# The opening of a decoder layer on one core: partial sums copied back into PSUM, every pair of tiles turned by transfers, conditioning one group earlier, x loaded by features, rows on GpSimd's queue

## The chip, the cores and the metric

The kernel runs on one core of one Trainium2 chip. The metric is the device time of one execution in microseconds. Engines are named as in the profile: PE is TensorE (matmuls and transposes), PEld its weight loads, DVE is VectorE, ACT is ScalarE, POOL is GpSimd and SP is SyncE, which issues most of the transfers. L12 is line 12 of the kernel.

## The reference

One layer: an adaLN-conditioned SwiGLU, token mixing (retention and sliding-window attention side by side), a second SwiGLU and a last norm, for 256 tokens of 2048 features, all in float32. The change touches the conditioning and the first SwiGLU:

```python
c_act = jax.nn.silu(c)
mod = (c_act @ w_ada[l] + b_ada[l]).reshape(b, N_MOD, D_MODEL)       # nine vectors of 2048
h = modulate(rms_norm(x, norm_ffn1[l]), mod[:, 0], mod[:, 1])         # h * (1 + scale) + shift
gate, up = jnp.split(h @ w_gu, 2, axis=-1)                            # w_gu: 2048 x 11264
x = x + 0.5 * mod[:, 2][:, None, :] * ((jax.nn.silu(gate) * up) @ w_down)
```

## The kernel before, in words

**Products.** A float32 product is made of three products of a shorter float type: the high part of the weights times the high part of the activations, high times low, and low times high (`products`, L349 to L363). ACT casts a weight tile to its high part (`wh`, L369), DVE subtracts that from the tile to get the low part (`wl`, L371). Both come two blocks at a time, 128x1024 numbers, into pools of three buffers each. The tiles themselves (`raw`, four buffers) are loaded by SP. Activations `h` are kept as `hh` (cast by ACT, L630) and `hl` (DVE, L631).

**The opening.** The first SwiGLU needs `h`, and `h` needs the conditioning vectors 0 and 1, which are products of silu(c) with 1 MB rows of `w_ada` (a row is a pair of vector number m and feature block k). The features are 16 blocks of 128. Rather than wait for all rows, the kernel begins with 16 chunks of 512 columns (eight pairs of a gate chunk and an up chunk) and goes over them in four groups of feature blocks: blocks 0 to 1, 2 to 5, 6 to 11 and 12 to 15 (L1114). Within a group every chunk is visited once (`visit`), which takes 12 matmuls for each two blocks. The order of the chunks is turned around in each group, and the last two chunks of a group keep their PSUM banks into the next. All others move their sums out: `to_parts` writes them to `part_of(n)` in SBUF, at the first time with an ACT copy (L1158), later with a DVE addition (L1155). In the last group `swiglu_up` adds the kept sums to the bank (L699, L700) and makes silu(gate) x up. The result is turned, for even pairs by PE transposes (L512) and an ACT copy (L513), for odd ones by two `flat` copies (L529), a transposing transfer (L534) and two copies back (L545). There are three `flat` buffers.

**What runs beside.** While the visits of one group run, the generator `group` prepares the blocks of the next: it loads rows (`place`, two row buffers in `ring` after the first rows), multiplies and sums them on DVE (`ada_pass`, L219: 128x2048 at once in the first group, two halves of 128x1024 later), ends the sums (`ada_end`, L237 to L244), scales x (`turned_x`, ACT, L1022), turns it by four PE transposes for each pair of blocks (L1026), modulates it (ACT, L622) and splits it into `hh` and `hl`. In the last group the rows of vectors 2, 4 and 3 begin (`set_pace`, 32 of their 192 quarter-row passes, 128x512 each); the rest follow in `ffn_up`.

**What sets the order.** Every engine takes its instructions in order. Which order that is follows from the program and from a scheduler, which places an instruction when it expects its inputs; `tc.issue_after` ties a copy to the newest cast. An instruction that waits holds up all behind it on its engine, and SP and POOL hold up the transfers behind a waiting one in the same way.

The pools that decide when buffers come free are these:

```python
raws = ctx.enter_context(tc.tile_pool(name="raws", bufs=RAWS))
wsp = ctx.enter_context(tc.tile_pool(name="wsp", bufs=3))
flat = ctx.enter_context(tc.tile_pool(name="flat", bufs=3))
psa = ctx.enter_context(tc.tile_pool(name="psa", bufs=4, space=PSUM))
psm = ctx.enter_context(tc.tile_pool(name="psm", bufs=2, space=PSUM))
psd = ctx.enter_context(tc.tile_pool(name="psd", bufs=2, space=PSUM))
```

A visit takes two banks of `psa`, so two chunks are in PSUM at a time.

## Time and profile before

| | |
|---|---|
| median of three runs | 2361.56 us (2360.13 to 2361.72) |
| the profiled execution | 2360.87 us, its span 2359.1 us |
| granted clock in the span | 0.999 |
| ACT, busy in the span | 1314.8 us |
| rows of `w_ada` loaded into `slot` buffers by SP | 83 of 1024 KB, median 7.0 us to landing |
| weight tiles of the SwiGLUs, by SP | 160 of 1024 KB, median 5.1 us to landing |

The opening is the first 450 us or so. A line of the windows view gives, for one stretch, the busy time of each engine with its count of instructions, then the granted clock of PE, the busy share of the DMA engines and what they moved. A line of the waits view gives the waiting instruction, who released it, and the total, the count and the longest of such waits. A line of the timeline gives start and duration, and in brackets the idle time before it with its releaser. In the chain, a line is a piece of the path that ended last.

### The profile page before, as it was taken

What the parts mean: (1) busy time and instruction counts of PE and PEld (TensorE: products, weight loads), DVE (VectorE), ACT (ScalarE), POOL (GpSimd) and SP (SyncE); (2) the same over time, 40 slices, a digit from 0 to 9 for tenths busy, and PEclk for the clock granted to TensorE, in tenths of its full rate; (3) what the DMA queues carried; (4) which work ended last, traced back from release to release, by engine and by line L of the source; (5) the groups of instructions that cost most, each with busy time, mean ns of one, the idle gap of its engine ahead of it and who ended that gap; (6) DMA issues with size and microseconds to landing.
All of it is one profiled execution on the core that took longest, in us unless ns stands there. A gap on an engine that the chain in (4) does not pass through costs nothing.

```text
span 2359.1 us, 28364 instructions
## 1 busy us (share of the span) xinstructions
PE 2338.8 (99%) x10479; PEld 1921.2 (81%) x10479; DVE 1697.5 (72%) x2628; ACT 1314.8 (56%) x1779; POOL 9.2 (0%) x21
## 2 busy tenths in 40 slices
PE   8999999999999999999999999999999999999998
PEld 5888888888888888778888888888888888888887
DVE  7987799779977768976777776676555555555656
ACT  6544466455556568774556564465455455455544
POOL 0000000000000000000000000000000000000000
PEclk9999999999999999999999999999999999999999
DMA  9987789999776889967678787754777777676553
GB/s 386 365 295 267 267 288 366 368 315 357 304 257 229 284 274 247 260 216 250 265 283 301 284 300 289 279 205 179 255 234 256 244 241 254 235 230 203 193 196 125
DMA packets 186316, 627.87 MB, mean 266 GB/s; under 512 B 108801, under 2 KB 109185, under 8 KB 115649
## 3 DMA queue, kind: packets, MB, share of 16 engines
q1 hardware_dynamic: 183682, 615.05, 74.9%
q0 software_dynamic: 1600, 9.83, 1.2%
q8 instruction: 82, 1.34, 0.2%
q10 hardware_dynamic: 896, 1.19, 0.1%
q14 instruction: 56, 0.46, 0.1%
HBM read 597.16 MB, written 4.22 MB: 255 GB/s over the span
## 4 chain that ended last, share of the span: by engine, by line
PE 97%; DMA 1%; DVE 1%; ACT 0%; issue 0%; SPq 0%; DVEq 0%; ACTq 0%
PE pa L355 95%; PE ps L1372 0%; DMA slot<-in_w_ada_dram 0%; DMA rows_x<-in_w_ada_dram 0%; PE pd L1288 0%; DVE slot L219 0%; DMA x_sb<-in_x_dram 0%; PE ps L355 0%; PE ps L888 0%; DVE wl L371 0%; PE ps L512 0%; ACT wh L369 0%; DVE rows_x L219 0%; PE ps L1288 0%; PE pd L1470 0%
## 5 line engine op out<-in xcount | busy, mean ns | idle before, releaser
L369 ACT CAST wh<-raw 128x1024 fp32r<-128x1024 f32 x792 | 831.1, 1054 | 883.3 <-PE pa L355 836.7
L371 DVE TENSOR_TENSOR wl<-raw,wh 128x1024 fp32r<-128x1024 f32 x792 | 960.8, 1222 | 478.0 <-ACT wh L369 416.6
L355 PE MATMUL pa<-wh,hh 128*128 128x512 f32 x2184 | 595.5, 392 | 2.2 <-ACT wh L369 1.6
L355 PE MATMUL pa<-wh,hl 128*128 128x512 f32 x2184 | 589.7, 389 | 0.0
L355 PE MATMUL pa<-wl,hh 128*128 128x512 f32 x2184 | 585.2, 390 | 0.4 <-DVE wl L371 0.3
L355 PEld LDWEIGHTS pa<-wh,hh 128*128 128x128 f32 x2184 | 407.3, 188 | 90.2 <-ACT wh L369 4.2
L355 PEld LDWEIGHTS pa<-wh,hl 128*128 128x128 f32 x2184 | 409.9, 188 | 86.3 <-issue 0.4
L355 PEld LDWEIGHTS pa<-wl,hh 128*128 128x128 f32 x2184 | 409.1, 188 | 87.0 <-DVE wl L371 1.3
L355 PE MATMUL pa<-wh,a 128*128 128x512 f32 x1824 | 452.4, 389 | 0.0
L355 PEld LDWEIGHTS pa<-wh,a 128*128 128x128 f32 x1824 | 341.6, 188 | 71.0 <-DVE a L405 0.4
L355 PE MATMUL pa<-wl,a 128*128 128x512 f32 x912 | 245.2, 389 | 0.0
L219 DVE CUSTOM_DVE_ANT_0 slot<-slot,cact 128x512 f32<-128x512 f32 (+2 forms) x272 | 209.5, 820 | 11.0 <-DMA slot<-in_w_ada_dram 10.8
L355 PEld LDWEIGHTS pa<-wl,a 128*128 128x128 f32 x912 | 171.1, 188 | 35.4
L219 DVE CUSTOM_DVE_ANT_0 rows_x<-rows_x,cact 128x512 f32<-128x512 f32 x124 | 78.8, 688 | 24.9 <-DMA rows_x<-in_w_ada_dram 24.9
L545 ACT COPY slot<-back 128x512 uint16<-128x512 uint16 x140 | 93.4, 767 | 0.0
L404 ACT CAST a<-slot 128x512 fp32r<-128x512 f32 x114 | 70.5, 620 | 28.3 <-PE pa L355 28.2
L219 DVE CUSTOM_DVE_ANT_0 raw<-raw,cact 128x512 f32<-128x512 f32 (+1 forms) x108 | 70.8, 708 | 20.3 <-DMA raw<-in_w_ada_dram 20.3
L405 DVE TENSOR_TENSOR a<-slot,a 128x512 fp32r<-128x512 f32 x114 | 78.0, 685 | 0.1
L529 ACT COPY flat<-t 128x512 uint16<-128x512 uint16 x128 | 72.1, 617 | 7.5 <-DVE t L1445 5.5
L1155 DVE TENSOR_TENSOR slot<-slot,pa 128x512 f32<-128x512 f32 x48 | 31.0, 683 | 16.7 <-PE pa L355 16.7
L219 DVE DVE_READ_ACCUMULATOR2_ANT sums<- 128x1 f32 x504 | 41.7, 83 | 0.0
L355 PE MATMUL pa<-wh,home 128*128 128x512 f32 x160 | 39.5, 389 | 0.0
(223 smaller groups left out, 1068.9 us busy)
## 6 DMA issues: line engine op xcount, KB each, us to landing
raw<-in_w_ffn_gu_dram SPq DMA_DIRECT2D x160, 1024.0 KB, 5.1
raw<-in_w_in_dram SPq DMA_DIRECT2D x104, 1024.0 KB, 6.4
raw<-in_w_ffn_down_dram SPq DMA_DIRECT2D x88, 1024.0 KB, 4.9
slot<-in_w_ada_dram SPq DMA_DIRECT2D x83, 1024.0 KB, 7.0
rows_x<-in_w_ada_dram SPq DMA_DIRECT2D x31, 1024.0 KB, 7.2
raw<-in_w_ada_dram SPq DMA_DIRECT2D x26, 1024.0 KB, 6.5
raw<-in_w_swa_branch_dram SPq DMA_DIRECT2D x16, 1024.0 KB, 6.1
raw<-in_w_ret_branch_dram SPq DMA_DIRECT2D x16, 1024.0 KB, 6.2
```

What stands on the lines that cost most here:

```text
L219: nc.vector.tensor_tensor_reduce(out=w[:, at], in0=w[:, at], in1=cact[:, at], scale=1.0, scalar=0.0, op0=ALU.mult, op1=ALU.add, accum_out= ...
L355: product = nc.tensor.matmul(banks[t], act[:, j, t * P : (t + 1) * P], weights[:, j, :], start=starts and i == 0 and j == 0, stop=ends and ...
L369: cast.append(nc.scalar.copy(hi, src).ins)
L371: low.append(nc.vector.tensor_sub(lo, src, hi.bitcast(F32)).ins)
L404: nc.scalar.copy(hi, v)
L405: nc.vector.tensor_sub(lo, v, hi.bitcast(F32))
L529: nc.scalar.copy(planes[:, i, :], words(src)[:, :, i])
L545: nc.scalar.copy(into[:, :, :, i], held["turned"][:, i])
L1155: nc.vector.tensor_add(p, p, b)
```

## The change

Five parts. (1) *Copied sums.* A chunk whose sums lie in SBUF has its two banks filled by ACT copies before its visit (seeds, L1172), the matmuls accumulate onto them, and `to_parts` always writes out with ACT copies; the additions of L1155 are gone. Chunks that are left to the last group are still added in `swiglu_up`. (2) All eight pairs are turned by transfers. (3) The 32 passes of vectors 2, 4 and 3 stand in the third group, with one row buffer for them, and the rows of the group itself then have one buffer too. (4) From block 6 on, x comes from a second copy of the input, laid out by features on the host (`x_t`); DVE multiplies it by the row of inverse norms (L1060), which one small matmul spreads over the partitions (L1053). (5) Rows of block 2 and up, and those of part 3, are loaded from GpSimd's queue.

```diff
@@ -207,11 +208,11 @@
 
     AQ = 4
 
-    def ada_load(m, k, w, loads=1):
+    def ada_load(m, k, w, loads=1, queue=nc.sync):
         src = w_ada[(m * KD + k) * P : (m * KD + k + 1) * P, :]
         for i in range(loads):
             at = slice(i * D // loads, (i + 1) * D // loads)
-            nc.sync.dma_start(w[:, at], src[:, at])
+            queue.dma_start(w[:, at], src[:, at])
 
     def ada_pass(k, w, sums, q, passes=AQ):
 
@@ -258,6 +259,10 @@
 
         return place
 
+    own_sums = [
+        small_c[:, C_COS : C_COS + KD * AQ].rearrange("p (k q) -> p k q", q=AQ)
+    ]
+
     def conditioning(outputs, place, behind):
 
 
@@ -265,13 +270,13 @@
         held = {}
         step = 0
         for m, gain, row in outputs:
-            sums = ada_sums()
+            sums = own_sums.pop() if own_sums else ada_sums()
             for k in range(KD):
                 for q in range(AQ):
                     for i in range(step // AQ, min((step + pace["ahead"]) // AQ + 1, len(tiles))):
                         if i not in held:
                             held[i] = place()
-                            ada_load(*tiles[i], held[i])
+                            ada_load(*tiles[i], held[i], 1, pace["queue"])
                     if behind is not None and step < 2 * AQ:
                         with tc.issue_after(behind.ins):
                             ada_pass(k, held[step // AQ], sums, q)
@@ -301,7 +306,7 @@
         return nc.gpsimd.dma_start(row, gate_d[m // 3][None, :].broadcast_to([P, D]))
 
 
-    pace = {"steps": iter(()), "rate": 0.0, "due": 0.0, "behind": None}
+    pace = {"steps": iter(()), "rate": 0.0, "due": 0.0, "behind": None, "queue": nc.gpsimd}
 
     def set_pace(outputs, halves, place, ahead):
         assert next(pace["steps"], None) is None
@@ -346,7 +351,7 @@
         nc.sync.dma_start(raw, w[c0 // CH, :, kb * KB : (kb + 1) * KB, :])
         return raw
 
-    def products(banks, ah, al, wh, wl, starts, ends, halves=range(NT)):
+    def products(banks, ah, al, wh, wl, starts, ends, halves=range(NT), seeded=False):
         n = ah.shape[1]
         parts = ((ah, wh), (al, wh), (ah, wl))
         for i, (act, weights) in enumerate(parts):
@@ -358,6 +363,7 @@
                         weights[:, j, :],
                         start=starts and i == 0 and j == 0,
                         stop=ends and i == 2 and j == n - 1,
+                        skip_group_check=seeded,
                     )
         newest.append(product.ins)
         del newest[:-1]
@@ -969,15 +975,19 @@
         return [part[(n - 2) // 4][:, at + t * CH : at + (t + 1) * CH] for t in range(NT)]
 
     early = [ada_sums() for _ in range(2)]
-    rows_of = {}
+    rows_of, alone = {}, [False]
 
     def place(m, k):
         if k < 1:
             rows_of[m, k] = raw_row()
         else:
-            ring.append(ring.pop(0))
-            rows_of[m, k] = ring[-1]
-        ada_load(m, k, rows_of[m, k], 2 if k < 2 else 1)
+            if not alone[0]:
+                ring.reverse()
+            rows_of[m, k] = ring[0]
+        if k < 2:
+            ada_load(m, k, rows_of[m, k], 2)
+        else:
+            ada_load(m, k, rows_of[m, k], 1, nc.gpsimd)
 
     firsts = (2 * EARLY - 1, 2 * EARLY - 2)
 
@@ -1028,9 +1038,34 @@
                 )
         return turned
 
+    TURNED = 6
+    root_rows = []
+
+    def roots_in_rows():
+
+        diag = t512()
+        for t in range(NT):
+            nc.scalar.mul(diag[:, t * P : (t + 1) * P], ident, r[:, t : t + 1])
+        full = flat_tile()[:, :P]
+        nc.gpsimd.memset(full, 1.0)
+        root_rows.append(side_bank()[:, :S])
+        with tc.issue_after(newest[-1]):
+            nc.tensor.matmul(root_rows[0], full, diag[:, :S], start=True, stop=True)
+
+    def normed_columns(k0):
+
+        xt = t512()
+        both = xt.rearrange("p (k s) -> p k s", s=S)
+        nc.sync.dma_start(both, x_t[k0 : k0 + 2].rearrange("k p s -> p k s"))
+        nc.vector.tensor_mul(
+            both, both, root_rows[0][:, None, :].broadcast_to([P, 2, S])
+        )
+        return [xt[:, i * S : (i + 1) * S] for i in range(2)]
+
     def group(ks, passes=2):
 
         for k0 in ks[::2]:
+            srcs = normed_columns(k0) if k0 >= TURNED else None
             for k in (k0, k0 + 1):
                 for m in (1, 0):
                     if (m, k) not in rows_of:
@@ -1041,11 +1076,11 @@
             for m in (1, 0):
                 ada_end(m, slice(k0, k0 + 2), early[m], 0 if m else None, passes)
             h = t512()
-            for i, src in enumerate(turned_x(k0)):
+            for i, src in enumerate(srcs or turned_x(k0)):
                 modulated(h[:, i * S : (i + 1) * S], k0 + i, src, 0)
             parts_of_h(held, k0, h)
 
-    banks, moved = {}, set()
+    banks, moved, unlinted = {}, set(), set()
     for n, one_bank in zip(firsts, (acc_bank, side_bank)):
         banks[n] = [one_bank() for _ in range(NT)]
 
@@ -1123,10 +1158,18 @@
         nc.sync.dma_start(raw[:, : len(ks), :], gu[c0 // CH, :, ks[0] : ks[-1] + 1, :])
         return raw
 
-    def visit(n, ks, ends, ticks=False):
+    def visit(n, ks, ends, ticks=False, ends_all=False):
         starts = n not in banks
+        seeded = starts and n in moved and not ends_all
         if starts:
             banks[n] = [acc_bank() for _ in range(NT)]
+        if starts:
+            unlinted.discard(n)
+        if seeded:
+            unlinted.add(n)
+            for b, p in zip(banks[n], part_of(n)):
+                with tc.issue_after(cast[-1]):
+                    nc.scalar.copy(b, p)
         raw_of = [(load_blocks(n, part), part) for part in (ks[:KB], ks[KB:]) if part]
         pieces = [
             (raw[:, a : a + 2, :], part[a : a + 2])
@@ -1143,19 +1186,17 @@
                 held.lo[:, hl, :],
                 wh,
                 wl,
-                starts and a == 0,
+                starts and a == 0 and not seeded,
                 b == len(ks) and ends,
+                seeded=n in unlinted,
             )
             if ticks:
                 tick()
 
     def to_parts(n):
         for p, b in zip(part_of(n), banks.pop(n)):
-            if n in moved:
-                nc.vector.tensor_add(p, p, b)
-            else:
-                with tc.issue_after(cast[-1]):
-                    nc.scalar.copy(p, b)
+            with tc.issue_after(cast[-1]):
+                nc.scalar.copy(p, b)
         moved.add(n)
 
     ROWS_FFN1 = [(2, None, 0.5), (4, 1, None), (3, None, None)]
@@ -1164,10 +1205,15 @@
     def place_row():
         return row_ring[0]() if row_ring else raw_row()
 
+    def place_early():
+        return row_ring[0]() if row_ring else ring[1]
+
     for g, ks in enumerate(groups):
+        alone.append(g == len(groups) - 2)
+        del alone[:-1]
         final = g == len(groups) - 1
-        if final:
-            set_pace(ROWS_FFN1, 32 * 192 // 32, place_row, 1)
+        if g == len(groups) - 2:
+            set_pace(ROWS_FFN1, 48 * 192 // 32, place_early, 0)
         order = chunks if (len(groups) - g) % 2 else chunks[::-1]
         coming = iter(()) if final else group(groups[g + 1], 1 if g == 0 else 2)
         due = 0 if final else 2 * len(groups[g + 1])
@@ -1175,7 +1221,7 @@
         for i, n in enumerate(order):
             if g == 0 and n in firsts:
                 continue
-            visit(n, ks, n not in stay, final)
+            visit(n, ks, n not in stay, g == len(groups) - 2, final or (g == len(groups) - 2 and n in stay))
             if final:
                 turn_step()
             last = len(order) - 2
@@ -1192,6 +1238,8 @@
                         to_parts(m)
                 if i == 3:
                     columns_rest()
+                if i == 5:
+                    roots_in_rows()
             if n in stay or g == 0:
                 continue
             if not final:
@@ -1203,11 +1251,12 @@
                     tiles,
                     n // 2,
                     (part_of(n - 1), part_of(n)),
-                    n // 2 % 2 == 1,
+                    True,
                 )
     gate = gate_row()
     tiles.append(slot())
     row_ring.append(two_rows())
+    pace["queue"] = nc.sync
     pace["rate"] = (192 - 32) / 117
     pace["ahead"] = AQ
     ffn_up(held, gu, tiles, EARLY, turned=range(EARLY, DFF // CH))
```

Three places of the order, each before and after. In the names, `wh` and `wl` are weight parts, `raw` their tile, `slot_8` holds two rows of `w_ada`, `sums_16` and `sums_15` are the sums of vectors 1 and 0, `pa` are PSUM banks, `back` and `slot_5` to `slot_6` keep partial sums.

DVE between the first and the second group, before: the rows of block 5 end early, and `hl_4` (here of blocks 4 and 5) stands between the weight parts.

```order
L219 ISA slot_8_117,sums_15_124<-slot_8_117,cact_103 128x2048 [waits DMAHW4_49]
L219 ISA sums_15_124 128x1
L242 TENSOR_TENSOR modc_106<-sums_15_124,bcols_105 128x2 [waits DVE_49]
L371 TENSOR_TENSOR wl_112_529<-raw_110_526,wh_111_528 128x1024 [waits DMAHW5_49,PE_49,Activation_49]
L371 TENSOR_TENSOR wl_117_551<-raw_115_548,wh_116_550 128x1024 [waits DMAHW6_49,PE_49,Activation_49]
L371 TENSOR_TENSOR wl_127_591<-raw_125_588,wh_126_590 128x1024 [waits DMAHW7_49,PE_49,Activation_49]
L631 TENSOR_TENSOR hl_4_113<-t_118_569,hh_3_112 128x512 [waits Activation_49]
L371 TENSOR_TENSOR wl_130_609<-raw_128_606,wh_129_608 128x1024 [waits DMAHW0_49,PE_49,Activation_49]
L371 TENSOR_TENSOR wl_132_625<-raw_128_606,wh_131_624 128x1024 [waits PE_49,Activation_49]
L371 TENSOR_TENSOR wl_135_645<-raw_133_642,wh_134_644 128x1024 [waits DMAHW1_49,PE_49,Activation_49]
L219 ISA slot_8_117,sums_16_125<-slot_8_117,cact_103 128x1024 [waits DMAHW2_49]
L219 ISA sums_16_125 128x1
```

The same place after the change:

```order
L377 TENSOR_TENSOR wl_138_652<-raw_136_649,wh_137_651 128x1024 [waits DMAHW1_49,PE_49,Activation_49]
L377 TENSOR_TENSOR wl_140_668<-raw_136_649,wh_139_667 128x1024 [waits PE_49,Activation_49]
L220 ISA slot_8_117,sums_16_125<-slot_8_117,cact_103 128x1024 [waits DMASW3_49]
L220 ISA sums_16_125 128x1
L220 ISA slot_8_117,sums_16_125<-slot_8_117,cact_103 128x1024
L220 ISA sums_16_125 128x1
L1060 TENSOR_TENSOR t_141_683<-t_141_683,pd_70_347 128x512 [waits DMAHW2_49]
L637 TENSOR_TENSOR hl_4_113<-t_121_576,hh_3_112 128x512 [waits Activation_49]
L220 ISA slot_8_117,sums_15_124<-slot_8_117,cact_103 128x1024 [waits DMASW4_49]
```

`hl_4` now stands behind two halves of row (1,6) and the multiply of x, and the row's transfer comes from GpSimd's queue (DMASW).

ACT at the beginning of the second group, before: one cast of chunk 2 (`wh_141`) stands ahead of the copies out of chunk 0 (`pa_123`, `pa_124`).

```order
L369 CAST wh_141_685<-raw_140_683 128x1024 [waits DMAHW3_49,DVE_49,PE_49]
L1158 COPY back_11_120<-pa_123_586 128x512 [waits PE_49]
L1158 COPY back_12_121<-pa_124_587 128x512 [waits PE_49]
L369 CAST wh_143_701<-raw_140_683 128x1024 [waits DVE_49,PE_49]
L1158 COPY back_13_122<-pa_113_546 128x512 [waits PE_49]
L369 CAST wh_148_726<-raw_147_724 128x1024 [waits DMAHW5_49,DVE_49]
L1158 COPY back_14_123<-pa_114_547 128x512 [waits PE_49]
L369 CAST wh_150_742<-raw_147_724 128x1024 [waits DVE_49,PE_49]
```

After, with `pa_126` and `pa_127` as the banks of chunk 0 and `pa_142` and `pa_143` as those of chunk 2:

```order
L636 CAST hh_3_112<-t_121_576 128x512 [waits Activation_49]
L1199 COPY back_11_120<-pa_126_593 128x512 [waits PE_49]
L1199 COPY back_12_121<-pa_127_594 128x512 [waits PE_49]
L375 CAST wh_145_697<-raw_144_695 128x1024 [waits DMAHW3_49,DVE_49]
L375 CAST wh_147_713<-raw_144_695 128x1024
L1172 COPY pa_142_691<-slot_5_114 128x512 [waits Activation_49]
L1172 COPY pa_143_692<-slot_5_114 128x512 [waits Activation_49]
L1199 COPY back_13_122<-pa_116_553 128x512 [waits PE_49]
L1199 COPY back_14_123<-pa_117_554 128x512 [waits PE_49]
```

The copies out come first, then both casts, then the seeds, which need the banks that the copies free.

ACT five chunks later, before: casts, the modulation of the next blocks, casts.

```order
L369 CAST wh_164_824<-raw_161_806 128x1024 [waits DVE_49,PE_49]
L622 ACTIVATE t_166_845<-ps_169_850,modc_106 128x256 [waits DVE_49]
L622 ACTIVATE t_166_845<-ps_170_851,modc_106 128x256
L1022 ACTIVATE t_207_1068<-x_sb_97,rs2_21_150 128x256
L1022 ACTIVATE t_208_1069<-x_sb_97,rs2_21_150 128x256
L630 CAST hh_3_112<-t_166_845 128x512 [waits Activation_49]
L369 CAST wh_174_869<-raw_173_867 128x1024 [waits DMAHW3_49,PE_49]
L369 CAST wh_176_885<-raw_173_867 128x1024 [waits PE_49]
```

After, `pa_163` and `pa_164` being chunk 5 and `raw_174` the weights of chunk 6:

```order
L1172 COPY pa_172_876<-slot_6_115 128x512 [waits Activation_49]
L1172 COPY pa_173_877<-slot_6_115 128x512 [waits Activation_49]
L628 ACTIVATE t_170_863<-t_141_683,modc_106 128x256 [waits DVE_49]
L628 ACTIVATE t_170_863<-t_141_683,modc_106 128x256
L636 CAST hh_3_112<-t_170_863 128x512 [waits Activation_49]
L1199 COPY slot_5_114<-pa_163_820 128x512 [waits PE_49]
L1199 COPY slot_5_114<-pa_164_821 128x512 [waits PE_49]
L375 CAST wh_175_882<-raw_174_880 128x1024 [waits DMAHW0_49]
L375 CAST wh_177_898<-raw_174_880 128x1024
```

The casts of chunk 6 now stand behind two copies that wait for PE's last matmul of chunk 5.

More of the change, by code (lines that the diff above doesn't have):

```diff
@@ L98, in layer_kernel @@
     consts,
+    x_t,
     out,
@@ L1665 @@
     given["w_ada"] = _np.asarray(given["w_ada"])[0].T
+    given["x_t"] = _np.asarray(given["x"])[0].T.reshape(KD, P, S)
     for name in _BY_CHUNK:
```

## The prediction

> **What bounds the kernel now.** The page comes first: how full each engine is, and which engine carries the chain that ends last.
>
> ```profile
> PE 2338.8 (99%) x10479; PEld 1921.2 (81%) x10479; DVE 1697.5 (72%) x2628; ACT 1314.8 (56%) x1779; POOL 9.2 (0%) x21
> PE 97%; DMA 1%; DVE 1%; ACT 0%; issue 0%; SPq 0%; DVEq 0%; ACTq 0%
> ```
>
> PE is busy for 2338.8 of 2359.1 us and carries 97% of the chain. So the time is PE's work plus PE's waits, and the change can pay in two ways only: fewer PE instructions, or shorter waits of PE. Next, PE's waits over the whole span, and the windows of the opening.
>
> ```profile
> PE ps L1026 <- ACT t L1022: 3.9, 1, 3.9
> PE pa L1064 <- ACT t L622: 2.8, 2, 1.8
> PE pa L176 <- DMA c_row<-in_c_dram: 2.7, 1, 2.7
> PE pa L355 <- ACT wh L369: 1.6, 3, 1.0
> core 0: us, PE busy (x) PEld busy (x) DVE busy (x) ACT busy (x) POOL busy (x), PEclk, DMA share, GB/s
> 25.00:60.00 35.00, 33.41 (x144) 25.35 (x143) 30.67 (x34) 25.15 (x41) 0.00 (x0) 1.00 1.01 405
> 60.00:100.00 40.00, 39.87 (x177) 32.52 (x176) 34.98 (x50) 23.83 (x34) 0.00 (x0) 1.00 0.95 369
> 100.00:150.00 50.00, 50.00 (x226) 41.42 (x225) 49.80 (x77) 21.88 (x25) 0.00 (x0) 1.00 0.86 329
> 300.00:350.00 50.00, 50.00 (x230) 41.53 (x230) 47.93 (x81) 30.26 (x38) 0.00 (x0) 1.00 0.88 283
> 350.00:400.00 50.00, 50.00 (x230) 41.58 (x229) 48.19 (x88) 33.94 (x46) 0.00 (x0) 1.00 1.03 357
> ```
>
> The reader is to see that the three largest waits belong to the first 25 us (input, first turned block, first modulated block), which the change leaves as they are, and that from 100 us on PE has no gap at all: 50.00 of 50.00, although DVE stands at 49.80. DVE is nearly full there, but it is not late. Taking its additions away pays nothing by itself; the 1.7 us that PE idles between 25 and 100 us are all the waits that could go.
>
> **What the change removes from PE.** The chain gives the transposes that PE does between products.
>
> ```profile
> 25.46 1.72 PE pd L1064 x4
> 103.25 0.44 PE ps L1026 x4
> 103.69 31.79 PE pa L355 x140
> 309.29 0.87 PE ps L512 x8
> ```
>
> A transpose costs 0.11 us of PE (0.44 / 4, 0.87 / 8) and a product's matmul 0.227 (31.79 / 140). Twenty transposes of x (blocks 6 to 15, two each) are 2.2 us, four pairs of eight transposes are 3.5. The one new matmul, 128x256 in plain f32, is half of the 0.43 of a 128x512 (1.72 / 4), 0.2. All of this stands where PE is full, so PE's work falls by 2.2 + 3.5 - 0.2 = **5.5 us**.
>
> **What it adds around PE.** Everything else runs on ACT, DVE and the queues, and counts only where PE comes to wait for it. Durations of the opening, grouped by shape (busy, mean ns), and then two stretches of the timeline:
>
> ```profile
> L371 DVE TENSOR_TENSOR wl<-raw,wh 128x1024 fp32r<-128x1024 f32 x141 | 170.3, 1220 | 32.2 <-ACT wh L369 28.3 <-PE pa L355 2.0 <-PE ps L1026 1.7
> L369 ACT CAST wh<-raw 128x1024 fp32r<-128x1024 f32 x141 | 148.4, 1055 | 176.9 <-PE pa L355 160.3 <-issue 4.8 <-DVE slot L1155 3.3
> L219 DVE CUSTOM_DVE_ANT_0 slot<-slot,cact 128x512 f32<-128x512 f32 x44 | 27.9, 687 | 0.0
> L1155 DVE TENSOR_TENSOR slot<-slot,pa 128x512 f32<-128x512 f32 x48 | 31.0, 683 | 16.7 <-PE pa L355 16.7
> L529 ACT COPY flat<-t 128x512 uint16<-128x512 uint16 x20 | 11.3, 615 | 0.2 <-DVE t L703 0.2
> L545 ACT COPY slot<-back 128x512 uint16<-128x512 uint16 x16 | 10.7, 770 | 0.0
> L513 ACT COPY slot<-ps 128x512 f32<-128x512 f32 x8 | 4.4, 588 | 0.9 <-PE ps L512 0.8
> ...
> 49.88 1.99 PE L355 MATMUL pa<-wl,hh 128*128 128x512 f32 x8
> 50.77 1.08 ACT L1158 COPY slot<-pa 128x512 f32<-128x512 f32 x2 [2.90 <-PE pa L355]
> 51.72 1.06 ACT L369 CAST wh<-raw 128x1024 fp32r<-128x1024 f32 x1
> 52.83 1.20 PE L355 MATMUL pa<-wh,hh 128*128 128x512 f32 x4 [0.97 <-ACT wh L369]
> ...
> 59.49 2.28 DVE L219 CUSTOM_DVE_ANT_0 slot<-slot,cact 128x2048 f32<-128x2048 f32 x1
> 61.71 0.08 DVE L219 DVE_READ_ACCUMULATOR2_ANT sums<- 128x1 f32 x1
> 63.77 2.00 ACT L369 CAST wh<-raw 128x1024 fp32r<-128x1024 f32 x2
> 64.85 2.36 DVE L371 TENSOR_TENSOR wl<-raw,wh 128x1024 fp32r<-128x1024 f32 x2 [1.70 <-PE ps L1026]
> 67.13 0.69 DVE L631 TENSOR_TENSOR hl<-t,hh 128x512 fp32r<-128x512 f32 x1
> 70.45 1.07 PE L355 MATMUL pa<-wh,hh 128*128 128x512 f32 x4
> ```
>
> *Seeds for additions.* 52 copies into PSUM and 52 copies out on ACT take the place of 52 additions on DVE. A copy of two is 1.08, so ACT gains about 56 us over groups 2 to 4 and DVE loses 52 x 0.68 = 35. A visit of the second group is 24 matmuls, 5.45 us of PE; its ACT work is two casts (2.0), two copies out (1.1) and two seeds (1.1), 4.2. It fits on average; what counts is the order at the edges.
>
> *Second chunk of the second group (B).* Chunk 2 takes the bank of chunk 0. On ACT stand, behind chunk 0's last matmul: two copies out (1.08), both casts of chunk 2 (2.0), one seed (0.54): 3.6. PE has only eight matmuls of chunk 1 left, 1.8. Before, one cast stood ahead of the copies and no seed behind them. Late by 1.8; the hand-overs can overlap a little, so between 1.2 and 1.8, I take **1.5**.
>
> *Chunk 6 of that group (C, D).* The cast of chunk 6's weights now stands behind the copies out of chunk 5, and these wait for PE's last matmul of chunk 5. The stretch at 50 us shows such a case: PE ends, two copies, one cast, PE starts 0.97 late even though PE still had part of its work when the copies were released. Here PE has none left: 1.08 + 1.06 = 2.1. Behind it the low part of the same weights stands on DVE behind two passes of a row (2.36) and the multiply of x (0.69, as hl of the same shape), which wait for that row. That is worth nothing if the row has landed, up to 3.9 if it comes a load late; I take 1.0, the end near to nothing, since rows of this group have 12 visits of slack. Together **3.1** (2.1 to 6.0).
>
> *Start of the second group (A).* The low part of blocks 4 and 5 (hl) is needed after 32 matmuls, 7.27 us into the group. On DVE it now stands behind the row (1,6) and the x multiply. Early bound: the third weight buffer comes free 12 matmuls in (2.72), then wl 1.18, row 2.36, multiply 0.69, hl 0.69: 7.64, so 0.4 late. Late bound: the last wl of the first group ends as before at 64.85 + 2.36 = 67.21, 3.24 ahead of the group (70.45); row (1,5) follows it now (2.36), then the load of row (1,6) into its buffer runs beside four wl and a row (4 x 1.18 + 2.36 = 7.08). With a load no longer than that, hl ends at -0.88 + 7.08 + 3.74 = 9.94, 2.7 late; with a load of 8.5 it is 4.1 late. The loads:
>
> ```profile
> slot<-in_w_ada_dram SPq DMA_DIRECT2D x10, 1024.0 KB, 6.6
> ...
> row<-gate_d POOLq DMA_DIRECT2D x3, 1024.0 KB, 9.1
> back<-flat SPq DMA_TRANSPOSE x70, 7.5
> dec<-in_consts_dram POOLq DMA_DIRECT2D x1, 1024.0 KB, 9.0
> gf<-in_norm_final_dram POOLq DMA_DIRECT2D x1, 1024.0 KB, 8.3
> ```
>
> Rows on SP's queue land in 6.6 us between 8 and 70 us; transfers of the same size on GpSimd's queue took 8.3 to 9.1, though in other stages and two of the three kinds repeat one row. ACT has lost two scalings at this place, so the casts will be earlier than before; I take **1.5**, nearer to the early bound (0.4 to 4.1). [...] No run here shows the two queues on the same transfer.
>
> *Fourth group (E, F).* Four more pairs go through the transfer: per pair four flat copies (0.62) and four copies back (0.77) for two copies of L513 (0.59), +4.4 us each, 17.5 in all, on an ACT that is busy for 30.26 + 33.94 = 64.2 of 100 us. It stays under full. But the three flat buffers come free when transfers land (7.5 us, more than a visit of 5.45), and casts stand behind flat copies that wait. In return the conditioning passes of this group are gone (DVE 48 of 50 before), which was no wait. Nothing at best; at worst two transfers are awaited with about 3 us each, 6. I take **3**.
>
> *Into ffn_up's end of the opening and the down product (G, H).* The copies back and the low parts of the last pairs come later and stand behind passes of the next rows (four are 2.7). 0 to 3.2, I take **2**.
>
> *Conditioning in the third group* costs DVE 32 passes of 0.69 (22 us) in a group of 131 us (16 visits of 36 matmuls) that loses 28 additions of 0.68 (19): covered. *x by transfers* adds five loads of 256 KB to queues that had room (DMA share 0.86 from 100 to 150 us) and takes scalings off ACT: covered. *Rows on GpSimd's queue* take 36 issues from SP, whose own wait was on no chain: worth nothing but what stands under A.
>
> **Sum.** 1.5 + 1.5 + 3.1 + 3 + 2 = 11.1 of waits less 5.5 of work: +5.6 on the profiled run of 2360.87, so 2366.5. The median of the runs shown is 2361.56, 0.7 above the profiled one: **about 2367**. With all bounds low: 0.4 + 1.2 + 2.1 - 5.5 = -1.8, with all high: 4.1 + 1.8 + 6.0 + 6.0 + 3.2 - 5.5 = +15.6.
>
> **The rivals.**
> 1. *Covered.* The scheduler's edges hurt less than the order shows: the engines run far enough ahead that copies and seeds meet free banks, and PE waits nowhere. Then only the 5.5 remains: 2356. For it: PE's perfect rows from 100 us on, with DVE at 49.8 of 50. Against it: in B and C the wait follows from the order on one engine, not from a load. This is the other side, and it decides if the new waits stay under 0.8 us.
> 2. *Half.* B and C's 2.1 happen, A stays at its early bound and E to H nearly cost nothing: 0.4 + 1.5 + 2.1 + 1.5 = 5.5 against 5.5: 2361.5, no difference.
> 3. *Late rows.* GpSimd's queue delivers a row in 10 us instead of 8.5 when everything moves at 400 GB/s. Then A's late bound becomes -0.88 + 10 + 3.74 - 7.27 = 5.6, 4 more than taken, and D goes to its end near 2: 2372. [...]
>
> **How the numbers follow.** Forecast (waits of 8 to 14 us, 2363.5 to 2370) 0.45, late rows or more (to 2377) 0.15, half 0.27, covered 0.13. A measurement of this kernel can tell about 0.2%, 4.7 us, from no change; so 2356.8 to 2366.3 counts as the same. Of the forecast's 0.45 some 0.1 lies under 2366.3; of covered 0.12 lies under 2356.8. Faster 0.12, same 0.38, slower 0.50. The range goes from 2357 to 2375: it leaves out most of the covered case and the end of the late rows. The likeliest case's own range is 2363.5 to 2370.
>
> **What would show it.** PE's busy time should fall by about 5.5 us with no L512 group left. PE's waits should name ACT (a cast or a copy into a bank) within the first 110 us with two single waits of 1.5 to 2.1, and DVE hl once. If PE's waits stay near the 12 us of before, rival 1 holds and steps B and C are wrong. If the pass group of the opening shows idle time before it that ends with a row's transfer, rival 3 is at work. The windows from 300 to 450 us should show PE below full; if they stay at 50.00, E to H were mis-sized.

## The result, and the profile after

| | before | after |
|---|---|---|
| median | 2361.57 us (2360.13 to 2362.01) | 2374.09 us (2373.06 to 2375.66) |
| profiled execution, its span | 2360.87, 2359.1 us | 2373.06, 2371.3 us |
| ratio to before, 95% interval | | 1.0057 (1.0046 to 1.0067) |
| PE busy | 2338.8 us | 2339.6 us |

The change makes the kernel 12.2 us slower, profiled execution against profiled execution. The forecast was +5.6. Of all executions in this document one stood far apart, with 4801.65 us, among the ten of the run with x by PE; it is in that run's median of 2362.05, which would be 2361.55 without it. First the page of after: its engines and its chain.

```profile
PE 2339.6 (99%) x10429; PEld 1919.0 (81%) x10429; DVE 1672.6 (71%) x2581; ACT 1375.3 (58%) x1899; POOL 28.5 (1%) x58
PE 92%; DMA 3%; DVE 2%; issue 2%; ACT 1%; SPq 0%; POOL 0%; ACTq 0%; DVEq 0%; POOLq 0%
```

DVE has lost work, ACT has gained 60 us, and PE has 50 instructions fewer (10429 for 10479). Yet PE is busy for 0.8 us *more*, and its share of the chain falls from 97% to 92%. So there are two losses: PE waits longer (span less busy time: 31.7 us, before 20.3), and PE's work itself has not become shorter. PE's waits over the whole span of after:

```profile
PE pa L360 <- DVE hl L637: 4.7, 1, 4.7
PE pa L360 <- DVE wl L377: 4.0, 4, 3.0
PE ps L1036 <- ACT t L1032: 3.8, 1, 3.8
PE pa L360 <- ACT wh L375: 3.3, 5, 1.9
PE pa L177 <- DMA c_row<-in_c_dram: 2.8, 1, 2.8
PE pa L1099 <- ACT t L628: 2.0, 2, 1.8
PE pa L360 <- DVE a L411: 1.1, 1, 1.1
PE pa L360 <- DVE t L643: 0.6, 1, 0.6
PE pa L360 <- DVE slot L1589: 0.6, 1, 0.6
PE pa L360 <- ACT pa L1172: 0.5, 1, 0.5
```

Three are new and large: 4.7 for hl, 3.0 for a low part of weights, 1.9 for a cast. The windows say where they lie (engine columns as before; the number behind the five engines is PE's granted clock).

```profile
25.00:60.00 35.00, 34.49 (x151) 26.86 (x150) 27.42 (x30) 25.34 (x42) 2.64 (x5) 1.00 0.95 362
60.00:100.00 40.00, 34.35 (x137) 26.90 (x136) 28.12 (x35) 22.99 (x34) 2.64 (x5) 0.91 0.94 372
100.00:150.00 50.00, 45.10 (x192) 36.51 (x191) 40.23 (x63) 34.90 (x53) 4.23 (x8) 0.97 0.89 339
150.00:200.00 50.00, 50.00 (x222) 41.44 (x221) 40.48 (x68) 31.94 (x46) 3.70 (x7) 1.00 0.85 314
76.38:79.79 3.41, 0.19 (x1) 0.00 (x0) 2.18 (x3) 0.00 (x0) 0.00 (x0) 1.00 1.01 423
79.79:86.62 6.83, 5.38 (x13) 4.22 (x14) 3.78 (x8) 1.99 (x4) 1.06 (x2) 0.50 1.01 416
113.93:117.34 3.41, 0.39 (x3) 0.12 (x2) 3.41 (x7) 1.12 (x3) 0.53 (x1) 1.00 0.40 103
117.34:120.75 3.41, 3.41 (x9) 2.64 (x10) 3.41 (x4) 0.96 (x1) 0.00 (x0) 0.50 0.87 353
```

The loss lies between 60 and 150 us; from 150 us PE is full again, but for five small waits between 400 and 1000 us, 3.1 us of idle time in all. And the granted clock, 1.00 in every window of before that was shown, is halved in two stretches: from 79.79 to 86.62 us, which begins inside the longest wait, and from 117.34 to 120.75 us, right behind the wait of 3.0. PE is busy for 5.38 and 3.41 us in them. Four matmuls take 2.07 us in the first of them (at 81.25 us) where four take 1.07 at clock 1.00, so about half of PE's busy time is lost, an estimate from these numbers: 2.7 + 1.7 = 4.4 us.

The largest wait in the timeline of after, around the start of the second group (at 68 us; DVE and PE, and the issue of the row that DVE waits for):

```profile
64.22 2.28 DVE L220 CUSTOM_DVE_ANT_0 slot<-slot,cact 128x2048 f32<-128x2048 f32 x1
66.80 0.53 POOL L215 DMA_DIRECT2D slot<-in_w_ada_dram  x1 [5.90 <-DVE modc L243]
...
77.61 1.23 DVE L220 CUSTOM_DVE_ANT_0 slot<-slot,cact 128x1024 f32<-128x1024 f32 x1 [2.98 <-DMA slot<-in_w_ada_dram]
78.76 1.22 DVE L220 CUSTOM_DVE_ANT_0 slot<-slot,cact 128x1024 f32<-128x1024 f32 x1
79.91 0.68 DVE L1060 TENSOR_TENSOR t<-t,pd 128x512 f32<-128x512 f32 x1
80.51 0.68 DVE L637 TENSOR_TENSOR hl<-t,hh 128x512 fp32r<-128x512 f32 x1
81.25 2.07 PE L360 MATMUL pa<-wh,hl 128*128 128x512 f32 x4 [4.67 <-DVE hl L637]
```

Row (1,5) is used up at 66.5, its buffer is loaded with row (1,6) from 66.80, and DVE can take that row at 77.61, 10.8 us later. The row, the multiply and hl follow, and PE starts 4.67 late. Four matmuls then take 2.07 us instead of 1.07.

### The profile page after: what moved, and what is told of

Its sections match the earlier page's. It is cut to its first block, busy times and chain, and to the rows that moved or that the text cites. A ratio compares the mean times of both kernels' runs of the same rounds, so it can differ in the third digit from the quotient of the medians.

```text
span 2371.3 us, 28338 instructions
## 1 busy us (share of the span) xinstructions
PE 2339.6 (99%) x10429; PEld 1919.0 (81%) x10429; DVE 1672.6 (71%) x2581; ACT 1375.3 (58%) x1899; POOL 28.5 (1%) x58
## 4 chain that ended last, share of the span: by engine, by line
PE 92%; DMA 3%; DVE 2%; issue 2%; ACT 1%; SPq 0%; POOL 0%; ACTq 0%; DVEq 0%; POOLq 0%
PE pa L360 90%; DMA raw<-in_w_ffn_gu_dram 2%; DMA slot<-in_w_ada_dram 1%; DVE slot L220 1%; ACT wh L375 1%; DVE wl L377 1%; PE ps L1421 0%; PE pd L1337 0%; ACT slot L551 0%; PE ps L360 0%; DMA t<-in_b_ada_dram 0%; PE ps L894 0%; ACT flat L535 0%; PE ps L1337 0%; PE pd L1521 0%
## 5 line engine op out<-in xcount | busy, mean ns | idle before, releaser
L220 DVE CUSTOM_DVE_ANT_0 slot<-slot,cact 128x512 f32<-128x512 f32 (+2 forms) x308 | 232.3, 803 | 15.8 <-DMA slot<-in_w_ada_dram 15.7
L551 ACT COPY slot<-back 128x512 uint16<-128x512 uint16 x156 | 104.0, 766 | 0.0
L535 ACT COPY flat<-t 128x512 uint16<-128x512 uint16 x144 | 81.3, 617 | 7.0 <-DVE t L1494 5.6
L220 DVE CUSTOM_DVE_ANT_0 raw<-raw,cact 128x512 f32<-128x512 f32 (+1 forms) x72 | 47.9, 715 | 10.8 <-DMA raw<-in_w_ada_dram 10.8
L1199 ACT COPY slot<-pa 128x512 f32<-128x512 f32 x72 | 38.6, 588 | 11.8 <-PE pa L360 11.7
L220 DVE DVE_READ_ACCUMULATOR2_ANT sums<- 128x1 f32 x440 | 35.8, 81 | 0.0
```

The lines of the kernel that those rows point to most:

```text
L220: nc.vector.tensor_tensor_reduce(out=w[:, at], in0=w[:, at], in1=cact[:, at], scale=1.0, scalar=0.0, op0=ALU.mult, op1=ALU.add, accum_out= ...
L535: nc.scalar.copy(planes[:, i, :], words(src)[:, :, i])
L551: nc.scalar.copy(into[:, :, :, i], held["turned"][:, i])
L1199: nc.scalar.copy(p, b)
```

## The experiments

All times are medians, beside the kernel before on the same chip. The runs used three chips, on which before has 2360.7, 2360.8 and 2361.0 us. Readings of waits and windows are those of each run's profiled execution.

**Each part undone alone.** Rows on SP's queue again (part 5):

```diff
-            ada_load(m, k, rows_of[m, k], 1, nc.gpsimd)
+            ada_load(m, k, rows_of[m, k], 1)
-    pace = {..., "queue": nc.gpsimd}
+    pace = {..., "queue": nc.sync}
```

> The change with part 5 undone: the rows from block 2 on and those of the third group are loaded from SP's queue again. In this build hl of blocks 4 and 5 stands ahead of row (1,6) on DVE again. Theory (order): the wait of 4.7 us for hl goes, with the slow matmuls behind it (about 3 us), the wait of 1.9 for the casts of chunk 6 stays: 2365 to 2368. Rival (the seeds and copies on ACT are what costs): 2373 or more.

Measured: 2365.68 us, ratio 1.0021 (1.0011 to 1.0030). PE has no wait between 60 and 100 us. The loads in the same stretch, 55 to 90 us, of after and then of this run (median us from issue to landing):

```profile
raw<-in_w_ffn_gu_dram SPq DMA_DIRECT2D x7, 1024.0 KB, 13.2
slot<-in_w_ada_dram POOLq DMA_DIRECT2D x6, 1024.0 KB, 9.2
```

```profile
raw<-in_w_ffn_gu_dram SPq DMA_DIRECT2D x7, 1024.0 KB, 8.8
slot<-in_w_ada_dram SPq DMA_DIRECT2D x5, 1024.0 KB, 6.8
```

In this stretch both land later with the rows on the second queue, 9.2 and 13.2 us against 6.8 and 8.8 (in before, on one queue, 8.2 for rows and 9.6 for weight tiles). How the transfers share the engines, these lines do not show. The wait of 1.9 at chunk 6 stays, and there is a twin of it 29 us later:

```profile
103.97 2.01 ACT L375 CAST wh<-raw 128x1024 fp32r<-128x1024 f32 x2
105.09 1.19 PE L360 MATMUL pa<-wh,hh 128*128 128x512 f32 x4 [1.88 <-ACT wh L375]
...
132.41 1.07 ACT L1199 COPY slot<-pa 128x512 f32<-128x512 f32 x2 [2.83 <-PE pa L360]
133.37 2.01 ACT L375 CAST wh<-raw 128x1024 fp32r<-128x1024 f32 x2
134.48 1.39 PE L360 MATMUL pa<-wh,hh 128*128 128x512 f32 x4 [1.88 <-ACT wh L375]
135.66 1.91 PE L360 MATMUL pa<-wh,hl 128*128 128x512 f32 x4
```

Copies out, cast, PE: the pattern of step C, 1.88 both times. Behind the first the matmuls run at full speed, behind the second at half (1.91 for four).

x of all blocks by ACT and PE (part 4):

```diff
-    TURNED = 6
+    TURNED = 16
-                if i == 5:
-                    roots_in_rows()
```

> The change with part 4 undone: x of all blocks is scaled by ACT and turned by PE. Theory: part 4's multiply and its early modulation are what bring row passes ahead of hl and of the low part of chunk 6, and the copies ahead of chunk 6's cast; all three waits (4.7 + 1.9 + 3.0) go, and the slow clock behind them (about 6), while PE gets 2 us of transposes back: 2359 to 2363. Rival (late rows on GpSimd's queue cost this much wherever they stand): the waits move and the time is 2372 to 2377.

Measured: 2362.05 us, 1.0005 (0.9995 to 1.0015). All three large waits are gone and the clock stays at 1.00, with the rows still on GpSimd's queue: between 60 and 100 us PE waits 2.2 in all. The rows land even later here, 10.0 us behind their issue in the stretch from 55 to 90 us. So neither part alone makes the wait for hl; parts 4 and 5 do it together.

hl tied ahead of the row, queue and transfers unchanged:

```diff
-        nc.vector.tensor_sub(held.lo[...], h, held.hi[...].bitcast(F32))
+        lo = nc.vector.tensor_sub(held.lo[...], h, held.hi[...].bitcast(F32))
+        h_low.append(lo.ins)
...
+        with tc.issue_after(h_low[-1]):
             nc.vector.tensor_mul(...)
...
+                        if k == ks[0] and passes > 1:
+                            with tc.issue_after(h_low[-1]):
+                                ada_pass(...)
```

> The change, with the multiply of x and the first row of a group tied behind the newest hl on DVE; queue and transfers stay as they are. Theory (order): the wait for hl goes with its slow clock, the row's own lateness costs at most 2 at the next weights: 2366 to 2370. Rival (the row's landing on GpSimd's queue is the cause): the wait moves from hl to the low part of chunk 2 at the same size, 2373 to 2375.

Measured: 2373.11 us, 1.0052 (1.0037 to 1.0067). The wait for hl is gone, but nothing is won; the rival was right in time and place, though not in size. PE's waits of this run between 60 and 100 us:

```profile
PE pa L360 <- DVE wl L377: 3.3, 2, 2.9
PE pa L360 <- ACT pa L1179: 1.5, 1, 1.5
PE pa L360 <- ACT wh L375: 1.0, 2, 0.6
```

DVE waits for the same row (until 77.89) and for the next (until 82.86), and now the weights of chunk 2 stand behind them. The seeds of chunk 2 come 1.5 late, what step B had priced; in after the wait for hl had hidden them. That the time is equal is partly chance: between 60 and 100 us PE idles for 5.8 us, in after for 5.7, and the slow clock there costs 1.5 instead of 2.7. Against that, a cast at 434 us comes 1.88 late here, with a slow stretch of its own (1.7), which after does not have.

Additions for seeds (part 1 undone):

```diff
-        seeded = starts and n in moved and not ends_all
+        seeded = False
...
+            if n in moved:
+                nc.vector.tensor_add(p, p, b)
+            else:
```

> The change with part 1 undone: sums are added by DVE, no seeds. Theory (order around rows): hl still stands behind row (1,6), so the 4.7 and its slow clock stay; the seed wait of 0.5 goes, DVE is fuller: 2372 to 2376. Rival (seeds and copies are what costs): below 2368.

Measured: 2369.72 us, 1.0037 (1.0024 to 1.0050), between the two expectations. The wait for hl stays (5.2), the 3.0 and the seeds' 0.5 go, a cast waits 2.5. So the seeds have a share of the loss in the second group, by the order that they bring, but not the largest.

**On SP's queue, with more undone.** Conditioning in the last group (parts 5 and 3):

```diff
...
-        alone.append(g == len(groups) - 2)
+        alone.append(False)
...
-        if g == len(groups) - 2:
-            set_pace(ROWS_FFN1, 48 * 192 // 32, place_early, 0)
+        if final:
+            set_pace(ROWS_FFN1, 32 * 192 // 32, place_row, 1)
...
-            visit(n, ks, n not in stay, g == len(groups) - 2, ...)
+            visit(n, ks, n not in stay, final, ...)
```

> The change with parts 5 and 3 undone: rows on SP's queue, and the conditioning of vectors 2, 4 and 3 in the last group. Against part 5 undone alone (2365.7). Theory: part 3 is what leaves small waits behind the opening (a low part of the down product behind four passes, 1.1, and two waits of 1.0 in all between 600 and 1000 us); the sum is 2 lower, 2363 to 2364.5. Rival: ACT in the last group is what is full, and passes beside it bring PE's casts later: 2366 to 2369.

Measured: 2362.90 us, 1.0009 (1.0000 to 1.0018), 2.8 lower. The wait at the down product is gone; the ones between 600 and 1000 us are not (0.99 us of idle time, as with part 3), so they were not part 3's. They are there with part 2 alone on the kernel before (0.98), and half as long with parts 5 and 2 undone (0.49). The two waits of 1.88 are there, and in this profile neither slows the clock. In the run with part 5 undone the slow clock costs 1.7 us, so only about 1.1 of the 2.8 is left for part 3.

Pairs turned by PE and by transfers in turn (parts 5 and 2 undone; the last argument of `swiglu_up` is `n // 2 % 2 == 1` again):

> The change with parts 5 and 2 undone: rows on SP's queue, and pairs turned by PE and by transfers in turn. Theory: the 32 transposes are worth 3.5 and all-by-transfers costs at most 2 in waits for casts in the last group and the low part of the down product, so it is 1.5 to 3.5 above part 5 undone alone: 2367 to 2369. Rival: waits for flat buffers cost what the transposes did: 2364 to 2366.

Measured: 2364.88 us, 1.0017 (1.0009 to 1.0026), 0.8 *below* part 5 undone alone, which the two intervals do not tell apart. The rival was right: the 3.5 us of transposes are paid for in full elsewhere.

Parts 2 and 4 alone on the kernel before:

> Parts 2 and 4 alone on the kernel before: all pairs by transfers, x by features from block 6, rows on SP's queue, additions, conditioning last. PE's work is the same 5.5 lower. Theory: without seeds and without the single row buffer the copies and the rows fit, waits of 3 to 5 come in, no slow clock: 2358.5 to 2361.5 beside 2360.8 of before. Rival (the early modulation of part 4 is enough to put casts late): 2364 or more.

Measured: 2361.26 us, 1.0002 (0.9993 to 1.0010). No large wait, no slow clock, and no gain.

Part 2 alone on the kernel before:

> Part 2 alone on the kernel before: all pairs are turned by transfers. PE's work falls by 3.5; waits of 1 to 3 in the last group and at the down product: 2358.5 to 2360.5 beside 2360.8. Rival: flat copies and transfers cost ACT as much as PE gains: 2361 to 2364.

Measured: 2361.21 us, 1.0003 (0.9994 to 1.0012). No gain; the expectation was 2358.5 to 2360.5, and the time is the rival's (2361 to 2364).

**Step C taken out.** On SP's queue, a chunk's sums go out after the next visit has been issued, so that its casts stand ahead of the copies:

```diff
             if not final:
-                to_parts(n)
+                waiting.append(n)
...
+            if g and not final:
+                for m in waiting:
+                    to_parts(m)
+                del waiting[:]
```

> Part 5 undone as before (2365.7), and the sums of a chunk are written out only when the next chunk's visit has been issued, so on ACT the casts of chunk 6 stand ahead of the copies out of chunk 5. Theory: the two waits of 1.9 for casts between 100 and 150 us go (3.8), with the slow stretch behind the second (1.7): 2359.5 to 2361. Rival: the seeds, which wait for those copies, become late instead: 2364 or more.

Measured: 2358.92 us, 0.9991 (0.9982 to 1.0000), 6.8 below the run without this edit. PE's idle time between 60 and 150 us falls from 3.9 to 0.1. Seeds are nowhere late.

> The same with the conditioning in the last group again (parts 1, 2 and 4, copies out later, rows on SP's queue). Theory: the small waits behind the opening go as in the run with parts 5 and 3 undone (2362.9), and here the 3.8 at chunk 6 goes too: 2358 to 2360, below the kernel before (2360.7). Rival as above: 2362 or more.

Measured: **2357.10 us**, 0.9984 (0.9975 to 0.9993). This is faster than both kernels: parts 1, 2 and 4 with the copies one visit later. Its page:

```profile
PE 2333.9 (99%) x10429; PEld 1916.4 (81%) x10429; DVE 1671.1 (71%) x2581; ACT 1374.3 (58%) x1899; POOL 9.4 (0%) x22
```

PE is busy for 4.9 us less than before; step by step, 5.5 had been worked out. Copies one visit later without seeds were not run, so how much of this is due to part 1 stays open; parts 2 and 4 without seeds and with the copies where they were had 2361.26.

> The run before it, with only the rows of blocks 2 to 5 on GpSimd's queue. Theory: the waits of the first group (1.6 to 1.9 between 25 and 60 us) shrink to 0.5 as in the change, and since hl stands ahead of row (1,6) the start of the second group costs at most 1: 2357 to 2359. Rival: the longer landing of rows beside weight tiles on two queues costs casts again: 2360 or more.

Measured: 2357.96 us, 0.9988 (0.9979 to 0.9997). Idle time between 25 and 60 us falls from 1.73 to 0.56, as it did in the change, but 2.2 us come in between 60 and 100, where at most 1 had been expected, and nothing is won over the run before it. The profiled execution was the slowest of the eleven (2360.21), so the 2.2 may be less in the others.

**The clock by itself.** Copies of h onto itself make PE wait at three places, with the kernel of 2357.10 us otherwise:

```diff
+            for _ in range({4: 11, 10: 22, 14: 38}.get(k0, 0)):
+                nc.scalar.copy(h, h)
             parts_of_h(held, k0, h)
```

> Copies out later, parts 5 and 3 undone, and in-place ACT copies of h (11 for blocks 4 and 5, 22 for blocks 10 and 11, 38 for blocks 14 and 15) that do nothing but make h late, so that PE waits about 2, 3.7 and 5.8 us at three places with no row or queue in it. Theory (a long wait slows the clock): the granted clock falls to about 0.5 to 0.7 for some 5 us behind the two longer waits, 1.5 to 2.5 lost each, and less or nothing behind the shortest. Rival (the slow clock belongs to the rows or the transfers): it stays at 1.00 behind all three.

Measured: 2381.82 us, 1.0090 (1.0071 to 1.0108). PE's first matmuls behind the three waits, in the timeline of this run:

```profile
78.87 3.51 PE L360 MATMUL pa<-wh,hh 128*128 128x512 f32 x8 [2.76 <-ACT hh L636]
...
178.12 3.69 PE L360 MATMUL pa<-wh,hh 128*128 128x512 f32 x8 [4.71 <-ACT hh L636]
181.65 1.08 PE L360 MATMUL pa<-wh,hl 128*128 128x512 f32 x4
...
312.63 3.78 PE L360 MATMUL pa<-wh,hh 128*128 128x512 f32 x8 [7.30 <-ACT hh L636]
316.21 1.91 PE L360 MATMUL pa<-wh,hl 128*128 128x512 f32 x4
```

Eight matmuls at full speed last 1.99 us, as in the prediction's rows; here 3.5 to 3.8. All three waits slow the clock, the shortest, 2.76, too, for which less or nothing had been expected. The stretches at half clock, from their first to their last moment:

```profile
79.20:82.61 3.41, 3.41 (x9) 2.62 (x8) 2.63 (x5) 0.00 (x0) 0.00 (x0) 0.50 1.01 423
178.18:181.60 3.42, 3.42 (x8) 2.72 (x9) 2.84 (x4) 0.00 (x0) 0.00 (x0) 0.50 0.02 10
307.89:318.13 10.24, 5.50 (x13) 4.34 (x14) 2.07 (x7) 4.46 (x8) 0.00 (x0) 0.50 0.32 111
```

Half of PE's busy time in them is 1.7, 1.7 and 2.8 us, the loss. The third stretch begins while PE still waits. No row of `w_ada` is loaded from another queue than SP's in this kernel, so the slow clock of these three places comes with the wait.

## Why the prediction was wrong, and where it was right

The sign and the two main mechanisms were right, the size was not: +5.6 forecast, +12.2 measured. Ahead of 25 us PE is busy for 0.7 us more than before and idle for 0.7 less, which moves nothing. Behind 25 us the sum closes as follows: PE's work -5.5, idle time +12.1 (23.0 against 11.0), slow clock +4.4, and a rest of 1.2. For the rest there is an estimate: around a wait, PE loses more than the idle time that the view gives. Two groups of four matmuls around a wait of 0.49 in after show it:

```profile
415.82 1.07 PE L360 MATMUL pa<-wl,hh 128*128 128x512 f32 x4
417.38 1.19 PE L360 MATMUL pa<-wh,hh 128*128 128x512 f32 x4 [0.49 <-ACT wh L375]
418.41 1.08 PE L360 MATMUL pa<-wh,hl 128*128 128x512 f32 x4
```

From 415.82 to 418.41 are 2.59 us for eight matmuls, 1.82 at full pitch: 0.77 lost where 0.49 is booked, so 0.28 for the hand-over. PE's list of waits counts 18 after and 9 before (the seven of the prediction's lines and two of 0.6 and 0.3). The 1.2 us are 0.13 for each of the nine more, half of what this one wait shows. So the hand-over is of the right size and no more; it was not tried by itself, and that it makes up the rest is not shown.

*The step that failed* is the first one, "the time is PE's work plus PE's waits", in which a wait costs its own length. The sum of waits nearly came out (11.1 forecast, 12.1 more idle time), but by luck, since errors of its terms cancel (A and D too small, B and E to H too large, as below). And no price stood in it for PE's work that a wait makes slower: 4.4 for the clock and the rest of 1.2, together 5.6 of the 6.6 by which the forecast missed.

- *PE's work.* Right: from 150 to 400 us, PE full in both, the products counted are 1083 before and 1104 after; 21 x 0.227 = 4.8 of the 5.5 lie there. The version of 2357.10 us shows 4.9 in the page.
- *A* was mis-sized, 1.5 for 4.7. The order was read rightly, but the early bound was taken where the late one held: row (1,5) ran 3.9 us ahead of the group, not earlier, and the next row took 10.8 us where the worst price in the sum was 8.5. That is rival 3, priced at 5.6 and called unlikely, with a chance of 0.15 that was the author's estimate and that no run had shown; its 2372 is the nearest of the four cases. Between the two queues, which no run ahead of the result had shown on the same transfer, the rows' landing differed by 2.4 us between 55 and 90 us (9.2 in after, 6.8 with part 5 undone). The cause is not the queue alone (x by PE removes the wait with the rows on that queue), nor the order alone (hl first only moves it): it is a row that lands late and a scheduler that puts work for PE behind it.
- *B* took 0.5 for 1.5, hidden behind A; with hl first it is 1.5.
- *C* was right, 1.9 for 2.1, and with the copies moved it goes.
- *D* was mis-sized, 3.0 for 1.0, for A's reason: rows of the second group have slack on average, but DVE stood waiting for one that it could take 8.4 us after its issue (104.61 to 113.05; issue, row and PE's wait in after):

```profile
104.61 0.54 POOL L215 DMA_DIRECT2D slot<-in_w_ada_dram  x1 [3.21 <-DVE modc L238]
113.05 1.22 DVE L220 CUSTOM_DVE_ANT_0 slot<-slot,cact 128x1024 f32<-128x1024 f32 x1 [3.36 <-DMA slot<-in_w_ada_dram]
117.22 1.99 PE L360 MATMUL pa<-wl,hh 128*128 128x512 f32 x4 [3.02 <-DVE wl L377]
```

- *E to H* were too dear: 1.0 between 400 and 450 us and 1.1 at the down product, for 5. From 300 to 400 us PE stays at 50.00 of 50 us; ACT, busy for 33 to 39 of 50 us between 300 and 450, is hardly late. The 1.0 between 600 and 1000 us had no term in the sum.
- *Rows on GpSimd's queue are worth nothing* was wrong in the other direction: idle time between 25 and 60 us is 0.5 in after, in the run with x by PE and with only the first rows there, and 1.7 to 1.9 in the runs with the rows on SP's queue and the seeds kept. For the first group's rows the queue was worth about 1.1.
- *Covered* (rival 1) is not this kernel, but near what the version of 2357.10 us is: 3.9 below before, with 0.9 more idle time than before.

## What to carry to other kernels

Read from the order what stands behind a wait, and price three things: the wait, the hand-over (0.13 to 0.28 us here, an estimate), and the clock behind it (1.5 to 2.8 us each time that it fell here). Work taken off a full PE did not pay by itself here: parts 2 and 4 took off 5.5 us and gained nothing alone (1.0002). Each copy that waits for PE's last matmul should stand behind the casts for its next (6.8 us here). The second queue was here a gain in one stretch and a loss in another. Between 20 and 60 us, with the rows on GpSimd's queue, weight tiles of 512 KB landed in 6.3 us in after and in 7.3 in before, and PE waited 1.1 less from 25 us on (0.5 for 1.6); between 55 and 90 us rows and tiles landed later than with part 5 undone (9.2 and 13.2 instead of 6.8 and 8.8), and work for PE stood behind a row.

## What the runs showed of the hardware

The granted clock fell to half (0.50) at or behind a wait of PE. The traces show it in six runs, twelve times in their first 450 us, for 3.41 us or twice or three times that (6.83 behind the wait of 4.67 in after, 10.24 behind that of 7.30), and 1.5 to 2.8 us were lost each time, by the estimate of half of PE's busy time in the stretch. Within a run the slow stretches began a whole number of times 3.413 us apart: 37.55 us, 11 times, in after; 98.99 and 129.71 us, 29 and 38 times, in the run with copies of h. So in these runs they lie on a raster of 3.413 us that runs on from one wait to the next, and whether the clock fell went by how busy PE was in the last piece of it, not by how long the wait was. The two waits of 1.88 in the run with part 5 undone show it:

```profile
101.18:104.59 3.41, 2.02 (x9) 1.33 (x8) 1.00 (x2) 1.58 (x3) 0.00 (x0) 1.00 1.01 389
131.90:135.31 3.41, 1.53 (x8) 0.94 (x7) 0.85 (x1) 2.90 (x5) 0.00 (x0) 1.00 0.82 259
135.31:138.72 3.41, 3.41 (x10) 2.63 (x9) 3.41 (x5) 3.10 (x5) 0.00 (x0) 0.50 0.85 358
```

The first wait (103.21 to 105.09) is cut in two by the raster, and PE was busy for 2.02 us of the piece that has the longer part of it; the second (132.60 to 134.48) lies in one piece, PE was busy for 1.53 us, and the next piece is slow. In the six runs, from 30 us on, every piece at full clock in which PE was busy for 1.53 us or less is followed by a slow one, and none in which it was busy for 1.81 or more (1.83 and 2.28 us in the pieces at 110.51 and 533.75 us of after). Single waits of 2.76 us (the first in the run with copies of h) and of 1.88 us, shorter than a piece, were enough. Where no stretch is slow the raster can't be placed, as in the run in which neither wait of 1.88 slowed the clock. The first 25 us are not counted: their rows give the clock as 1.00, though the first four plain f32 matmuls of before last 3.54 us and later ones 1.88.
